# Hybrid streaming encoder step: the norm weight by one transfer into all partitions, first weight casts on other engines, late probabilities scaled on VectorE

## The chip, the cores and the metric

The kernel runs on one core of one Trainium2 chip. The metric is the device time of one launch in microseconds (us), the median of several runs; lower is better. TensorE multiplies matrices, VectorE (DVE in the profile) and ScalarE (ACT) work elementwise and read the accumulators in PSUM, GpSimd (POOL) works elementwise on SBUF, and SyncE (SP) issues nearly all transfers.

## The reference

One inference step of one layer over 2048 new frames of a prompt and 64 frames of a running stream, width 1024, all in float32:

```python
xn = rms_norm(x, ln_g)                       # ln_g: one weight per column, 1024 of them
aq, ak, av, ag, hq, hf, hi, hg = split(xn @ w_in)      # w_in 1024 x 4096, eight parts of 512 columns
# group A: 8 heads of 64, each chunk of 64 frames sees 576 keys, with a bias by distance
o_a = softmax(aq @ ak.T / 8 + bias) @ av * silu(ag)
# group B: 4 heads of 128, gated linear recurrence; lb comes from lb_gamma by a softmax
f = lb + (1 - lb) * sigmoid(hf)
S_t = diag(f_t) S_(t-1) + (1 - f_t) i_t^T ;  o_t = S_t^T silu(hq_t)
o_b = rms_norm(o, norm_g) * silu(hg)
y = rms_norm(x + concat(o_a, o_b) @ w_out, ln_f_g)
```

## The kernel before

**Stages.** The 2112 rows are worked in four superblocks (`SUPER`) of 512, 576, 512 and 512 rows. For each, the rows are normed and transposed (`x_tile`, `x_split`), 32 jobs project them onto 128 columns of `w_in` each (`project`, job lists `JOBS`), and for each group of heads attention (`attention`, `softmax_rows`, `attend`) and the recurrence (`recurrence`, `rec_block`) run between the projections. The output projection (`out_step`) multiplies by seven combinations of the quarters of `w_out`; it starts while the last superblock's attention still runs.

**Precision.** Each float32 product is made of three faster ones: a value is cast to a high half and the rest is its low half. So `x_split` casts the transposed rows to `xh` on ScalarE and subtracts to get `xl` on VectorE, and `w_split` casts a weight tile (128 x 1024) to its high half and subtracts its low half in four quarters on POOL. `project` then makes three passes of eight products: high weight with `xh`, high weight with `xl`, low weight with `xh`. Probabilities are treated alike: transposed on TensorE (`tr`), cast on ScalarE and subtracted on VectorE into `ph` (`split_p`), then multiplied with V (`pv`).

**Order.** Every piece is a generator ("thread"). A planner (`Plan`) runs them against an estimated clock: `yield "D", t` means go on when the estimated VectorE queue is near time t, `yield lambda: ...` means go on when a condition holds, and the set `have` carries marks that others wait for. What comes out is one fixed order of instructions for each engine; on the chip each engine runs its own in that order and waits at semaphores. A piece that is written later in the plan therefore stands later in its engine's queue, and a changed estimate can change the order of everything after it.

**The start.** `program()` issues the first transfers on SyncE: x tile 0, the norm weight `ln_in_g` as one row of 4 KB into partition 0 of `g_in` (the rest of `g_in` was filled with zeros by VectorE), x tile 1, weight 0, and so on. TensorE runs idle products with the identity (`spinning`, output `g`). When the row is there, two products of 512 columns with a matrix of ones spread it over all partitions into two PSUM banks, `s` and `pv` (each is two instructions in the trace); VectorE scales the first x tiles by row factor and by these banks (`scalar_tensor_tensor`, 512 columns at a time), and after the four tiles ScalarE copies the banks into `g_in` for the later superblocks. Each tile's row factor is a square with a row sum, a logarithm and an exponential on ScalarE. The first weight is cast by POOL, the next three by VectorE. The first two projections (`hq`, `hf` of head 0) run in halves of 256 rows.

**The forget bounds.** `forget_bounds` works out `lb` and `oml` in seven tiny instructions on VectorE and one exponential on ScalarE. The mark "bounds" is set after the first three of them, and `ev_f`, which evacuates the forget gate's accumulator `hf` (a first exponential on ScalarE frees it), waits for that mark.

**Late probabilities.** `softmax_exp` takes the exponential with its row sum on ScalarE, inverts the sum on VectorE, and scales the row by it on VectorE, as a `tensor_scalar`. After the mark "parts" (set by `out_rows_g` once the last superblock's recurrence is done, from where the output projection has its first weights) the scaling is done on ScalarE. That is the case for the last eight of them, 640 columns each.

Of the kernel before, what the change touches and what calls it, by code (L numbers as in the profile page):

```python
# [17 lines left out]
P = 128  # L18
# [354 lines left out]
def hymba_step(  # L373
# [110 lines left out]
    def forget_bounds():  # L484

        yield lambda: x_laid(0, 0, 1)
        yield "D", 0.0
        lmx = T(cst, [P, NHB], F32, "lmx")
        le = T(cst, [P, 2, NHB], F32, "le")
        dve.tensor_tensor(lmx, lbg[:, 0], lbg[:, 1], ALU.max)  # L490
        for i in range(2):
            dve.tensor_sub(le[:, i], lbg[:, i], lmx)
        t = C.dve()
        have.add("bounds")
        yield "A", t
        act.activation(le, le, AF.Exp)
        yield "D", C.act()
        dve.tensor_add(lmx, le[:, 0], le[:, 1])
        dve.reciprocal(lmx, lmx)
        dve.tensor_mul(lb, le[:, 0], lmx)  # L500
        dve.tensor_scalar(oml, lb, -1.0, 1.0, ALU.mult, ALU.add)
        sp.dma_start(g_norm, hg_norm_g)


# [36 lines left out]


    x_there = {}
    x_left = {(-1, 0): True, (-1, 1): True}

    def x_tile(sb, half, c, here=None, gain=None):
# [12 lines left out]
        ss = T(wk, [P, 1], F32, "ss", bufs=4)  # L559
        yield "A", t  # L560
        yield from tk["ck"].get()
        junk = T(wk, [P, D], mybir.dt.bfloat16, "ck", bufs=1)
        act.activation(junk[:rows], xn[:rows], AF.Square, accum_out=ss[:rows])
        tk["ck"].put()
        r = rstd_of(ss, rows, D)
        t = C.act()
        if (sb, c) == (0, P):
            have.add("factors")
        if not sb:
            yield lambda: "gain" in have and (not half or x_laid(0, 0, 1))  # L570
        yield "D", t
        t = []
        for k0 in (0, 4) if gain else (0,):
            cs = slice(k0 * P, k0 * P + (512 if gain else D))
            g = gain[k0 // 4] if gain else g_in[:rows]
            dve.scalar_tensor_tensor(xn[:rows, cs], xn[:rows, cs], r[:rows], g, ALU.mult, ALU.mult)
            t.append(C.dve())
        yield lambda: x_left.get((sb - 1, half), False)
        ends = []
        for k0 in (0, 4):  # L580
            yield t[min(k0 // 4, len(t) - 1)]
            tags = ("g", "tr") if sb else ("acc", "tr", "g", "pv")
# [12 lines left out]
        if (sb, half, c) == (0, 0, P):  # L595
            have.add("rows")
# [57 lines left out]

    def w_split(j, nt, raw, t, tok):
        yield "P", t
        yield lambda: j == 0 or j - 1 in w_at
        if j in (1, 2):
            yield lambda: x_laid(0, j - 1, 1) and "bounds" in have
        yield from tk["w"].get()  # L660
        w = w_pair()
        if j == 0:
            pool.tensor_copy(w[:, 0], raw)
            t = C.pool(700, t)
        else:
            dve.tensor_copy(w[:, 0], raw)
            t = C.dve(540, t)
        th = t
        yield "P", t
        for k in range(0, KT, 2):  # L670
            pool.tensor_sub(w[:, 1, k : k + 2], raw[:, k : k + 2], f32(w[:, 0, k : k + 2]))
            t = C.pool(320, t)
            if k == 0:
                w_at[j] = [w, th, []]
            w_at[j][2].append(t)
            if k < KT - 2:
                yield "P", t - 100.0
# [363 lines left out]
    def softmax_exp(s, nm, nk, out, t):  # L1041
        sm = T(wk, [P, 1], F32, "sm", bufs=4)
        act.activation(s[:, :nk], s[:, :nk], AF.Exp, bias=nm[:, 0:1], scale=-1.0, accum_out=sm)
        t = C.act(nk + 300, t)
        yield "D", t
        dve.reciprocal(sm, sm)
        t = C.dve()
        if "parts" in have:
            yield "A", t
            act.activation(s[:, :nk], s[:, :nk], AF.Copy, scale=sm)  # L1050
            t = C.act()
        else:
            dve.tensor_scalar(s[:, :nk], s[:, :nk], sm, None, ALU.mult)
            t = C.dve()
        out.append((s, t))

    def vcols(v, t, h, rows):
# [269 lines left out]
    def head_jobs(sb, h):  # L1327
# [18 lines left out]

        def ev_f(acc, off, bn, t):
            c = slice(off, off + bn)
            yield lambda: "bounds" in have and front()
            yield from tk["sig"].get()  # L1350
            yield "A", t
            f = T(wk, [P, 512], F32, "sig", bufs=2)
            act.activation(f[:, :bn], acc, AF.Exp, scale=-1.0)
            tk["acc"].put(1, C.act())
            act.activation(f[:, :bn], f[:, :bn], AF.Ln, bias=one_t)
            act.activation(f[:, :bn], f[:, :bn], AF.Exp, scale=-1.0)
            t = C.act(3.4 * bn, t)
# [12 lines left out]
            r.t = max(r.t, t)  # L1370
# [662 lines left out]
    def program():  # L2033


        dve.memset(g_in, 0.0)
        constants()
        kroom = f32(T(pa, [P, 2, WIN + NMAX], F32R, "kd")).rearrange("p a c -> p (a c)")
        vroom = f32(T(pa, [P, 9, 4, 64], F32R, "v")).rearrange("p t s d -> p (t s d)")
# [6 lines left out]
        landed = {}  # L2046
        for what, i in (("x", 0), ("g", 0), ("x", 1), ("w", 0), ("x", 2), ("w", 1), ("x", 3), ("b", 0), ("w", 2),
                        ("w", 3)):
            if what == "g":
                sp.dma_start(g_in[0:1], ln_in_g.rearrange("(o d) -> o d", o=1))  # L2050
            elif what == "b":
                sp.dma_start(lbg, lb_gamma)
            elif what == "x":
# [4 lines left out]
        for i in range(4):  # L2058
            raws[i] = (wr0[i], landed["w", i], "raw" if i < 2 else None)
        spin = psum("g")  # L2060
        gps = [s_ps()[:, 0], psum("pv")]
        tk["g"].take()
        tk["s_ps"].take()
        tk["pv"].take()
        C.now = 600.0
        C.free["P"] = 4000.0

        def first_x():
            for c in range(4):
                C.spawn(x_tile(0, c // 2, c * P, (xr0[c], landed["x", c]), gps), 0)  # L2070
            yield lambda: x_laid(0, 1, 1)
            tk["xn"].put(3, C.now)
            yield "A", C.now
            for a, tag in enumerate(("s_ps", "pv")):
                act.copy(g_in[:, a * 512 : a * 512 + 512], gps[a])
                tk[tag].put(1, C.act())
            for a in (f32(ql[64:128, 0]), f32(ql[0:64, 1]), asb[1]):
                yield "P", 0.0
                pool.memset(a, 0.0)
                C.pool(300)  # L2080
            yield lambda: 3 in w_at
            tk["kv"].put()
# [5 lines left out]
        C.spawn(first_x(), 0)  # L2088
        C.spawn(forget_bounds(), 1)
        C.spawn(weights(), 2)  # L2090
        for _ in range(7):
            spinning()
            yield None

        for a in range(2):
            pe.matmul(gps[a], f32(ones), g_in[:, a * 512 : a * 512 + 512], start=True, stop=True)
            yield None
        have.add("gain")
        while "rows" not in have:
            spinning()  # L2100
            yield None
# [190 lines left out]
```

## Time and profile before

| | us |
|---|---|
| median of 3 runs (lowest to highest) | 1266.81 (1264.8 to 1267.21) |
| the profiled execution | 1267.05 |
| its span, first to last instruction | 1265.3 |
| TensorE busy | 1245.4 |
| VectorE, ScalarE, POOL busy | 891.5, 707.4, 375.2 |

A line of the profile names engine, operation, output <- inputs, shape and count, then time; in a timeline the first number is the start, the second how long the merged instructions ran, and the bracket is the engine's idle time before them and what ended it. A row of waits has the sum, the count and the longest. A row by windows has, for each stretch, the busy us of TensorE, of its weight loads, of VectorE, ScalarE and POOL with instruction counts, then the granted clock, the share of the DMA engines and GB/s. All helpers record one line of the code (L266), so names of tiles tell operations apart.

### The profile page before, as it was taken

What the parts mean: (1) busy time and instruction counts of PE and PEld (TensorE: products, weight loads), DVE (VectorE), ACT (ScalarE), POOL (GpSimd) and SP (SyncE); (2) the same over time, 40 slices, a digit from 0 to 9 for tenths busy, and PEclk for the clock granted to TensorE, in tenths of its full rate; (3) what the DMA queues carried; (4) which work ended last, traced back from release to release, by engine and by line L of the source; (5) the groups of instructions that cost most, each with busy time, mean ns of one, the idle gap of its engine ahead of it and who ended that gap; (6) DMA issues with size and microseconds to landing.
All of it is one profiled execution on the core that took longest, in us unless ns stands there. A gap on an engine that the chain in (4) does not pass through costs nothing. (4 is left out here: it accounts for less than half of the span.)

```text
span 1265.3 us, 22177 instructions
## 1 busy us (share of the span) xinstructions
PE 1245.4 (98%) x8120; PEld 1084.0 (86%) x8120; DVE 891.5 (70%) x1854; ACT 707.4 (56%) x1548; POOL 375.2 (30%) x687
## 2 busy tenths in 40 slices
PE   8999999999999999999999999999999999999997
PEld 7788887899999999998888888998888888788786
DVE  6786869766857668687584748784848574578886
ACT  5363546665645557575565656763636454753443
POOL 6766665111110110101634635110101104451110
PEclk9999999999999999999999999999999999999999
DMA  7877777655353464545879597646363657886331
GB/s 258 318 271 248 262 274 279 219 180 199 128 191 127 166 214 157 190 153 193 277 244 313 210 352 257 235 147 234 127 229 117 228 187 272 317 282 207 125 133 67
DMA packets 94830, 271.72 MB, mean 215 GB/s; under 512 B 10305, under 2 KB 43073, under 8 KB 77058
## 3 DMA queue, kind: packets, MB, share of 16 engines
q1 hardware_dynamic: 94722, 270.31, 60.7%
q8 instruction: 64, 1.05, 0.3%
q14 instruction: 44, 0.36, 0.1%
HBM read 186.66 MB, written 83.62 MB: 214 GB/s over the span
## 5 line engine op out<-in xcount | busy, mean ns | idle before, releaser
L266 PE MATMUL acc<-xh,w 128*128 128x512 f32 (+2 forms) x2720 | 567.4, 347 | 1.0 <-ACT sig L266 0.8
L266 PEld LDWEIGHTS acc<-xh,w 128*128 128x128 f32 x2720 | 436.1, 189 | 52.2 <-issue 1.9
L266 PE MATMUL acc<-xl,w 128*128 128x512 f32 (+2 forms) x1360 | 298.0, 348 | 0.0
L266 PEld LDWEIGHTS acc<-xl,w 128*128 128x128 f32 x1360 | 219.6, 189 | 24.8 <-issue 0.5
L266 POOL TENSOR_TENSOR mixa<-mixa,sga 128x256 f32<-128x256 f32 (+1 forms) x36 | 30.2, 840 | 352.1 <-DVE mixa L266 279.9
L266 DVE CUSTOM_DVE_ANT_0 pr<-s,bias 128x640 f32<-128x640 f32 (+5 forms) x144 | 100.7, 703 | 35.3 <-PE s L266 34.8
L266 ACT ACTIVATE pr<-pr,nm 128x640 f32<-128x640 f32 (+4 forms) x132 | 100.8, 763 | 38.2 <-DVE nm L266 37.2
L266 ACT CAST ph<-tr 128x512 fp32r<-128x512 f32 (+3 forms) x176 | 88.1, 508 | 60.1 <-PE tr L266 29.0
L266 POOL TENSOR_TENSOR w<-wraw,w 128x256 fp32r<-128x256 f32 x120 | 105.4, 907 | 48.4 <-DVE w L266 32.7
L266 DVE TENSOR_TENSOR ph<-tr,ph 128x512 fp32r<-128x512 f32 (+3 forms) x176 | 100.9, 589 | 9.4 <-ACT ph L266 8.2
L266 PE MATMUL pv<-ph,v 128*128 128x256 f32 (+2 forms) x344 | 97.5, 373 | 3.1 <-DVE ph L266 2.4
L266 PE MATMUL tr<-ident,pr 128*128 128x128 f32 x580 | 90.8, 273 | 1.8 <-DVE sig L266 0.7
L266 PEld LDWEIGHTS tr<-ident,pr 128*128 128x128 f32 x580 | 70.3, 140 | 16.0 <-issue 3.8
L266 ACT ACTIVATE sig<-acc 128x256 f32<-128x256 f32 (+2 forms) x86 | 42.8, 498 | 72.9 <-PE acc L266 72.6
L266 DVE TENSOR_SCALAR pr<-pr,sm 128x640 f32<-128x640 f32 (+3 forms) x124 | 68.6, 553 | 4.4
L266 DVE TENSOR_TENSOR mixa<-mixa,pv 64x256 f32<-64x256 f32 (+1 forms) x144 | 56.8, 394 | 20.8 <-ACT mixa L266 16.7
L266 ACT COPY vT<-acc 128x512 f32<-128x512 f32 (+2 forms) x64 | 31.2, 488 | 66.6 <-PE acc L266 66.5
L266 PEld LDWEIGHTS pv<-ph,v 128*128 128x128 f32 (+1 forms) x344 | 57.3, 189 | 10.9 <-issue 2.0
L266 ACT ACTIVATE sig<-sig 128x512 f32<-128x512 f32 (+2 forms) x109 | 57.3, 527 | 10.0 <-DVE gk L266 7.3
L266 POOL TENSOR_TENSOR k<-ob 128x512 f32<-128x512 f32 (+2 forms) x20 | 17.8, 891 | 145.4 <-ACT ob L266 145.4
L266 PE MATMUL s<-kd,q 128*128 128x320 f32 (+3 forms) x232 | 56.9, 315 | 0.1
L266 POOL TENSOR_TENSOR xn<-wraw,xn 128x256 fp32r<-128x256 f32 x48 | 37.8, 803 | 61.9 <-ACT xn L266 61.8
(315 smaller groups left out, 2100.7 us busy)
## 6 DMA issues: line engine op xcount, KB each, us to landing
w<-wd SPq DMA_DIRECT2D x96, 1024.0 KB, 5.0
wd<-w SPq DMA_DIRECT2D x32, 1024.0 KB, 7.3
wraw<-in_w_in_dram SPq DMA_DIRECT2D x30, 512.0 KB, 5.4
wod<-xn SPq DMA_DIRECT2D x28, 512.0 KB, 4.2
xn<-in_x_prompt_dram SPq DMA_DIRECT2D x23, 512.0 KB, 5.5
bias<-biasd SPq DMA_DIRECT2D x12, 640.0 KB, 7.1
carry<-kd SPq DMA_DIRECT2D x12, 512.0 KB, 7.9
carry<-v SPq DMA_DIRECT2D x12, 512.0 KB, 5.3
```

Of the source, the lines that this page charges most:

```text
L266: r = f(*args, **kw)
```

## The change

Three things, in one change:

1. The norm weight is read by one transfer with a source step of zero into all 128 partitions of `g_in` (512 KB written), after x tile 1 instead of before it. The zero fill, the four products, the two PSUM banks held for them and the two copies into `g_in` go. The first four tiles are scaled from `g_in` in SBUF, still in two halves.
2. The first weight's cast goes from POOL to VectorE, after the scaling of the second x tile (mark "scaled"). The third and fourth weights' casts go from VectorE to ScalarE. The evacuation of the forget gate waits, in the plan, for a new mark "lb", set when `lb` and `oml` are written.
3. After "parts", the scaling of probabilities is a VectorE `tensor_tensor` with the inverse sum spread along the row by a step of zero, in place of ScalarE's copy with a scale.

```diff
         dve.tensor_scalar(oml, lb, -1.0, 1.0, ALU.mult, ALU.add)
+        have.add("lb")
...
-            yield lambda: "gain" in have and (not half or x_laid(0, 0, 1))
+            yield lambda: not half or x_laid(0, 0, 1)
+            t = max(t, landed["g", 0])
         yield "D", t
         t = []
-        for k0 in (0, 4) if gain else (0,):
-            cs = slice(k0 * P, k0 * P + (512 if gain else D))
-            g = gain[k0 // 4] if gain else g_in[:rows]
-            dve.scalar_tensor_tensor(xn[:rows, cs], xn[:rows, cs], r[:rows], g, ALU.mult, ALU.mult)
+        for k0 in (0,) if sb else (0, 4):
+            cs = slice(k0 * P, k0 * P + (D if sb else 512))
+            dve.scalar_tensor_tensor(xn[:rows, cs], xn[:rows, cs], r[:rows], g_in[:rows, cs], ALU.mult, ALU.mult)
             t.append(C.dve())
+        if (sb, c) == (0, P):
+            have.add("scaled")
...
-        yield lambda: j == 0 or j - 1 in w_at
+        yield lambda: j - 1 in w_at if j else "scaled" in have
         if j in (1, 2):
             yield lambda: x_laid(0, j - 1, 1) and "bounds" in have
         yield from tk["w"].get()
         w = w_pair()
-        if j == 0:
-            pool.tensor_copy(w[:, 0], raw)
-            t = C.pool(700, t)
+        if j in (2, 3):
+            yield "A", t
+            act.copy(w[:, 0], raw)
+            t = C.act()
         else:
             dve.tensor_copy(w[:, 0], raw)
-            t = C.dve(540, t)
+            t = C.dve()
...
         if "parts" in have:
-            yield "A", t
-            act.activation(s[:, :nk], s[:, :nk], AF.Copy, scale=sm)
-            t = C.act()
+            dve.tensor_tensor(s[:, :nk], s[:, :nk], sm.to_broadcast([P, nk]), ALU.mult)
         else:
             dve.tensor_scalar(s[:, :nk], s[:, :nk], sm, None, ALU.mult)
-            t = C.dve()
+        t = C.dve()
...
-            yield lambda: "bounds" in have and front()
+            yield lambda: "lb" in have and front()
...
-        dve.memset(g_in, 0.0)
...
-        for what, i in (("x", 0), ("g", 0), ("x", 1), ("w", 0), ("x", 2), ("w", 1), ("x", 3), ("b", 0), ("w", 2),
+        for what, i in (("x", 0), ("x", 1), ("g", 0), ("w", 0), ("x", 2), ("w", 1), ("x", 3), ("b", 0), ("w", 2),
                         ("w", 3)):
             if what == "g":
-                sp.dma_start(g_in[0:1], ln_in_g.rearrange("(o d) -> o d", o=1))
+                sp.dma_start(g_in, ln_in_g.rearrange("(o d) -> o d", o=1).broadcast_to([P, D]))
...
-        gps = [s_ps()[:, 0], psum("pv")]
-        tk["s_ps"].take()
-        tk["pv"].take()
...
-            yield "A", C.now
-            for a, tag in enumerate(("s_ps", "pv")):
-                act.copy(g_in[:, a * 512 : a * 512 + 512], gps[a])
-                tk[tag].put(1, C.act())
...
-        for _ in range(7):
-            spinning()
-            yield None
-
-        for a in range(2):
-            pe.matmul(gps[a], f32(ones), g_in[:, a * 512 : a * 512 + 512], start=True, stop=True)
-            yield None
-        have.add("gain")
         while "rows" not in have:
             spinning()
             yield None
```

More of the change, by code (lines that the diff above doesn't have):

```diff
@@ L543, in hymba_step, with x_tile @@
     x_there = {}
+    landed = {}
     x_left = {(-1, 0): True, (-1, 1): True}
-    def x_tile(sb, half, c, here=None, gain=None):
+    def x_tile(sb, half, c, here=None):
         off, bn = SUPER[sb][3][half]
@@ L2045, in program @@
                 tk[tag].take()
-        landed = {}
-        for what, i in (("x", 0), ("g", 0), ("x", 1), ("w", 0), ("x", 2), ("w", 1), ("x", 3), ("b", 0), ("w", 2),
+        for what, i in (("x", 0), ("x", 1), ("g", 0), ("w", 0), ("x", 2), ("w", 1), ("x", 3), ("b", 0), ("w", 2),
                         ("w", 3)):
             if what == "g":
-                sp.dma_start(g_in[0:1], ln_in_g.rearrange("(o d) -> o d", o=1))
+                sp.dma_start(g_in, ln_in_g.rearrange("(o d) -> o d", o=1).broadcast_to([P, D]))
             elif what == "b":
@@ L2069, in first_x @@
             for c in range(4):
-                C.spawn(x_tile(0, c // 2, c * P, (xr0[c], landed["x", c]), gps), 0)
+                C.spawn(x_tile(0, c // 2, c * P, (xr0[c], landed["x", c])), 0)
             yield lambda: x_laid(0, 1, 1)
             tk["xn"].put(3, C.now)
-            yield "A", C.now
-            for a, tag in enumerate(("s_ps", "pv")):
-                act.copy(g_in[:, a * 512 : a * 512 + 512], gps[a])
-                tk[tag].put(1, C.act())
             for a in (f32(ql[64:128, 0]), f32(ql[0:64, 1]), asb[1]):
```

## The prediction

> **What bounds the kernel now.** I read the shares of busy time first, then the waits of TensorE, then the two places where the change works: the first 25 us and the stretch from 1075 to 1108 us. The page gives the shares:
>
> ```profile
> PE 1245.4 (98%) x8120; PEld 1084.0 (86%) x8120; DVE 891.5 (70%) x1854; ACT 707.4 (56%) x1548; POOL 375.2 (30%) x687
> ```
>
> TensorE is busy 98% of the span. The change takes away no product of the reference, so it can only gain where TensorE waits, or where what it does is filler. The waits of TensorE over the whole run begin like this (sum in us, times, longest):
>
> ```profile
> PE pv L266 <- DVE ph L266: 2.4, 2, 1.4
> PE g L266 <- POOL one L266: 1.4, 1, 1.4
> PE g L266 <- DVE xl L266: 1.2, 5, 0.4
> PE s L266 <- DMA gin<-in_ln_in_g_dram: 1.2, 1, 1.2
> PE g L266 <- DVE asb L266: 1.0, 1, 1.0
> PE acc L266 <- ACT sig L266: 0.8, 1, 0.8
> ```
>
> Two of these rows lie under the change: the gain's transfer (1.2) and the late products of the probabilities with V, which wait for VectorE's low halves `ph` (2.4 in two waits). At the start more is lost than waits show, because the idle products with the identity ("g") count as busy. The timeline of TensorE shows when real work begins:
>
> ```profile
> 5.97 2.05 PE L266 MATMUL s<-gin,ones 128*128 128x512 f32 x2 [1.18 <-DMA gin<-in_ln_in_g_dram]
> 7.80 1.92 PE L266 MATMUL pv<-gin,ones 128*128 128x512 f32 x2
> ...
> 13.40 1.19 PE L266 MATMUL acc<-xh,w 128*128 128x256 f32 x8 [0.28 <-issue]
> 14.43 1.12 PE L266 MATMUL acc<-xl,w 128*128 128x256 f32 x8
> ```
>
> The first projection starts at 13.40. What leads to it is VectorE's chain:
>
> ```profile
> 1.09 0.91 DVE L266 MEMSET gin<- 128x1024 f32 x1 [1.09 <-PEq L2279]
> ...
> 8.13 0.75 DVE L266 SCALAR_TENSOR_TENSOR xn<-xn,rstd,s 128x512 f32<-128x512 f32 x1 [5.11 <-PE s L266]
> 9.76 0.75 DVE L266 SCALAR_TENSOR_TENSOR xn<-xn,rstd,pv 128x512 f32<-128x512 f32 x1 [0.88 <-PE pv L266]
> 10.42 0.74 DVE L266 SCALAR_TENSOR_TENSOR xn<-xn,rstd,s 128x512 f32<-128x512 f32 x1
> 11.08 0.74 DVE L266 SCALAR_TENSOR_TENSOR xn<-xn,rstd,pv 128x512 f32<-128x512 f32 x1
> 12.02 1.29 DVE L266 TENSOR_TENSOR xl<-acc,xh 128x512 fp32r<-128x512 f32 x2 [0.19 <-ACT xh L266]
> 13.34 1.29 DVE L266 TENSOR_TENSOR xl<-tr,xh 128x512 fp32r<-128x512 f32 x2
> ...
> 14.88 0.69 DVE L266 CAST w<-wraw 128x1024 fp32r<-128x1024 f32 x1
> ```
>
> Four scalings, one every 0.66 us when nothing stops them, the last ending at 11.82; then four subtractions of low halves, one every 0.65 us, the last ending at 14.63. Between the first two scalings VectorE waits 0.88 us for the second half of the spread gain. So the start is set by when the gain stands in all partitions, and after that by VectorE.
>
> **Part 1, the gain.** Four products and a zero fill go; the gain now comes as 512 KB. SyncE's queue and ScalarE show the transfers before:
>
> ```profile
> 0.81 0.39 SPq L266 DMA_DIRECT2D xn<-in_x_prompt_dram  x1
> 2.03 0.31 SPq L266 DMA_DIRECT2D gin<-in_ln_in_g_dram  x1
> 2.39 0.35 SPq L266 DMA_DIRECT2D xn<-in_x_prompt_dram  x1
> ```
>
> ```profile
> 7.09 1.06 ACT L266 ACTIVATE ck<-xn 128x1024 bf16<-128x1024 f32 x1 [1.25 <-DMA xn<-in_x_prompt_dram]
> ...
> 20.45 0.59 ACT L266 COPY gin<-s 128x512 f32<-128x512 f32 x1
> 20.93 0.60 ACT L266 COPY gin<-pv 128x512 f32<-128x512 f32 x1
> 21.41 0.41 ACT L266 ACTIVATE sig<-acc 128x256 f32<-128x256 f32 x1
> ```
>
> ```profile
> 8.35 1.04 POOL L266 CAST w<-wraw 128x1024 fp32r<-128x1024 f32 x1 [4.75 <-DMA wraw<-in_w_in_dram]
> ```
>
> The gain's issue at 2.03 stood behind the zero fill (1.09 + 0.91 = 2.00), and the second tile of x and everything else on SyncE stood behind it. Without the fill the second x tile goes out where the first's issue ends, 0.81 + 0.39 = 1.2, or a little after: 1.1 us sooner. It landed at 7.09, so now at about 6.0, or nearer 5.3 if its bytes follow the first tile's without a pause. The first weight tile landed at 8.35, 1.26 after it: that is one 512 KB transfer at the rate of the row 7.00 to 8.50 below (columns at the right: clock, DMA share, GB/s). For a row of DRAM read into all partitions the trace has one case, the final gain:
>
> ```profile
> gin<-in_ln_f_g_dram SPq DMA_DIRECT2D x1, 512.0 KB
> ```
>
> ```profile
> 7.00:8.50 1.50, 1.50 (x3) 0.63 (x2) 0.37 (x1) 1.37 (x3) 0.15 (x1) 1.00 1.01 410
> 1075.50:1076.50 1.00, 1.00 (x6) 0.82 (x5) 0.75 (x2) 0.21 (x1) 0.00 (x0) 1.00 0.90 249
> 1076.50:1078.75 2.25, 2.25 (x14) 1.95 (x13) 0.98 (x3) 1.98 (x4) 0.00 (x0) 1.00 0.95 230
> ```
>
> It was issued behind a 256 KB store. The first stretch moves 0.25 MB, that store; the second moves 2.25 x 230 = 0.52 MB, the gain, with all engines of the DMA busy at little more than half the rate. I read the boundary from bytes and queue order, since no instruction marks it. So the gain takes 1.28 us at best and 2.25 us by its own kind. It lands between 5.3 + 1.28 = 6.6 and 6.0 + 2.25 = 8.2; I take 5.3 + 2.25 = 7.6, the rate of its own kind behind an x tile that no longer waits. The last of four scalings then ends at 7.6 + 3 x 0.66 + 0.75 = 10.3, 1.5 us earlier than 11.82. At 8.2 it is 0.9, at 6.6 it would be 2.5.
>
> **Part 2, the casts.** The first weight's high half leaves POOL (1.04) and goes to VectorE (0.69), behind the four scalings. Its transfer lands behind 512 KB more: between 8.35 - 1.1 + 1.28 = 8.5 and 8.35 + 2.25 = 10.6, about when VectorE gets there (10.3) or sooner. The cast ends at about 11.0, and POOL's four low quarters start after it and not at 9.4; they are wanted only in the third pass of the projection, two passes of about 1.0 us after the start, each by its own quarter, so I cost that at nothing. If POOL's train were late there, it would cost up to 0.7, one quarter. Since the cast stands ahead of the four subtractions, these end at 11.0 + 4 x 0.65 = 13.6 against 14.63: only 1.0 us earlier, while the first projection can start at 11.1, 2.3 earlier than 13.40, and then waits for the low halves. I take 1.4 us for TensorE from both, near VectorE's end, because after this VectorE has hardly a pause until 24 us. With the bounds of the landing: 0.4 to 2.2.
>
> The casts of the third and fourth weights move from VectorE to ScalarE. There is no such instruction in the trace; the nearest is the 1024-wide square at 7.09, 1.06 us, so about 2.1 us for both. The two copies of the gain (20.45 and 20.93, 0.48 apart) go. At 21.41 ScalarE reads the accumulator for which TensorE waits 0.8 us. One cast ahead of it stands for the two copies, no change; both ahead cost 1.1; none gives 0.2, what is left being the end of the product itself and the exponential. I take 0. The evacuation now also waits in the order until the forget bounds' last step is written; those are four tiny instructions on VectorE, so it costs nothing unless the order of the queue turns, which the 1.1 covers.
>
> **Part 3, the late probabilities.** Eight scalings by the inverse sum move from ScalarE to VectorE:
>
> ```profile
> L266 ACT ACTIVATE pr<-pr,sm x8: 814/830/832, 1077.4 to 1106.8; 128x640 f32<-128x640 f32 x8
> L266 DVE TENSOR_TENSOR pr<-pr,acc x7: 673/681/689, 1139.4 to 1258.7; 128x512 f32<-128x512 f32 x7
> ```
>
> ```profile
> 1093.21 1.55 ACT L266 ACTIVATE pr<-pr,sm 128x640 f32<-128x640 f32 x2
> ```
>
> ```profile
> 1092.00:1108.00 16.00, 14.57 (x77) 12.04 (x76) 8.61 (x22) 12.68 (x26) 12.55 (x21) 1.00 0.84 335
> ```
>
> ScalarE loses 8 x 0.83 = 6.6 us. VectorE gains 8 times a two-input instruction of 640 columns; the 512-column row is 0.681, so 0.681 x 640/512 = 0.85, together 6.8 us. In the windowed row (busy us of TensorE, its weight loads, VectorE, ScalarE, POOL) ScalarE works 12.68 of 16 and VectorE 8.61: the load goes from the fuller to the emptier queue. Both waits for `ph` (2.4 us together) stand behind ScalarE: VectorE subtracts what ScalarE has cast, and ahead of that an addition needs a bank that ScalarE copies. At the second wait two scalings, 1.55 us, stood in ScalarE's queue ahead of those casts. I expect half of the 2.4 to go, 1.2 us: the bank cannot be copied before its product has ended, so not all of it goes unless the order changes too. Bounds: 2.4 gained; below nothing, 1.5 lost, if a scaling (0.85) stands ahead of the subtraction in both places and costs most of its length.
>
> A rule that speaks against this part stands behind a row. The same VectorE operation of two inputs in SBUF takes two times:
>
> ```profile
> L266 DVE TENSOR_TENSOR q<-q,gq x3: 673/674/1229, 35.0 to 150.0; 128x512 f32<-128x512 f32 x3
> ```
>
> The Trainium skill, "SBUF — State Buffer", section "SBUF: two separate sides", says that VectorE with two SBUF inputs and GpSimd reading SBUF exclude each other for a whole instruction; the 1229 beside 673 agrees, and by it this part would lose instead of gain.
>
> **The sum.** The profiled execution took 1267.05 us, its span being 1265.3. Start 1.4, casts two and three 0, late part 1.2: 2.6 us less, 1264.45. The median of the runs shown is 1266.81, 0.24 below the profiled one, so 1264.2. The order of every queue is worked out by the kernel's own planner from estimated times, so all of it may shift a little; the smaller waits in the rows above show what one change of order is worth, 0.2 to 1.2 us, either way. I put 1.2 us either way on the sum for that.
>
> **The rivals.**
>
> *Hidden (no measurable change).* The start's gain is taken back. TensorE waits for the recurrence (DVE asb, 1.0); if that chain doesn't come sooner, TensorE only reaches it sooner and waits longer. For it: VectorE, not the gain, feeds the first projections. Against: the recurrence's own inputs come from the same shifted products. Then 0.4 of the 1.4 is left, and with 0.5 of the late 1.2: 1267.05 - 0.24 - 0.9 = 1265.9.
>
> *Slower: VectorE and POOL shut each other out late.* From 1092 to 1108 POOL works 12.55 of 16 us; before 1088 it is nearly idle, so this touches the last four of the eight scalings. By the row 673/674/1229 an instruction of that kind grows by up to 0.56, and POOL's subtraction behind it waits for 0.85. The place is the second wait for `ph`. Each of four scalings ahead of the subtraction then costs 0.85 + 0.56 = 1.4 on VectorE's chain. VectorE has 16 - 8.61 = 7.4 us free there and would use 5.6 of it, so it decides only if the scalings stand right before the subtractions for which TensorE waits. Then the 1.2 turns into 4 x 1.4 = 5.6 less the free time in front of two of them (2 x 0.9) = 3.8 lost; with the start's 1.4: 1266.8 + 2.4 = 1269.2. It decides once two of the four stand so.
>
> *The broadcast doesn't pay.* The transfer could be worse than its late sister, behind three others at once. Landing at 9.5 would put the last scaling at 12.2, later than 11.82. Start then -0.4 and, with the cast ahead of the subtractions, up to 1.0 lost; with late 1.2 gained: 1266.6.
>
> **How the numbers follow.** What measurements of this kernel can tell from no change is about 0.2%, 2.5 us. Both parts pay, as in the sum: 0.52, and that is faster by just over 0.2%, with more room below than above, since the landing's better bound (2.2) and both waits for `ph` (2.4) are worth 0.8 + 1.2 more. Hidden: 0.24, and the broadcast that doesn't pay: 0.08, both within. The lock, or an order that turns against the kernel by as much: 0.16, slower. The range: 0.8 + 1.2 + 1.2 below 1264.2 is 1261.0, taken as 1261.2; above it reaches to the lock's 1269.2, taken as 1269.0.
>
> **What would show it.** In the changed profile: the first scaling on VectorE at 7.6 (6.6 to 8.2), four of them without the 0.88 pause; the first projection at 11.1 to 11.9 and its low pass at 13.0 to 13.6; the cast of `w` on VectorE behind the scalings; 1024-wide casts of about 1.06 on ScalarE near 20; the wait of TensorE for `sig` still 0.7 to 0.9. Late: eight VectorE instructions of about 0.85, those after 1092 up to 1.4, and the waits for `ph` at 1.2 in sum. Wrong would be: a first scaling later than 9, a wait for `sig` of 1.5 or more, waits for `ph` above 2.4, or new waits between 25 and 1070 us that outweigh all of this.

## The result and the profile after

| | before | after |
|---|---|---|
| median of 22 runs each, same chip (us) | 1265.11 | 1267.74 |
| lowest to highest | 1263.73 to 1268.32 | 1266.33 to 1270.08 |
| the profiled execution, its span | 1267.05, 1265.3 | 1269.08, 1267.4 |

After to before: 1.0019, interval 1.0012 to 1.0026. The change is slower by 0.19%, some 2.4 us; the forecast was 2.6 us faster. The time lies in the stated range (1261.2 to 1269.0), the sign is the other one.

The page of after, shares of busy time (ScalarE has less, VectorE more, TensorE the same):

```profile
PE 1246.1 (98%) x8130; PEld 1085.9 (86%) x8130; DVE 903.7 (71%) x1862; ACT 703.2 (55%) x1540; POOL 375.9 (30%) x681
```

Waits of TensorE in after, whole run, the head of the list (sum, times, longest):

```profile
PE acc L266 <- DVE xn L266: 2.3, 2, 2.0
PE pv L266 <- ACT pr L266: 2.2, 1, 2.2
PE g L266 <- POOL one L266: 1.4, 1, 1.4
PE g L266 <- DVE xl L266: 1.2, 5, 0.4
PE g L266 <- DVE k L266: 1.2, 1, 1.2
```

Two rows are new. The gain's row and the `ph` row of before are gone; in their places stand a wait for the scaled x tile (2.0 at the start) and one of `pv` (2.2 near the end). Timelines of after, first VectorE and POOL, then TensorE, then SyncE's queue and ScalarE:

```profile
8.90 2.74 DVE L266 SCALAR_TENSOR_TENSOR xn<-xn,rstd,gin 128x512 f32<-128x512 f32 x4 [6.01 <-DMA gin<-in_ln_in_g_dram]
...
16.38 1.89 DVE L266 SCALAR_TENSOR_TENSOR xn<-xn,rstd,gin 128x512 f32<-128x512 f32 x2
18.20 2.37 DVE L266 SCALAR_TENSOR_TENSOR kd<-kd,rstd,gin 128x512 f32<-128x512 f32 x2
16.54 4.62 POOL L266 TENSOR_TENSOR w<-wraw,w 128x256 fp32r<-128x256 f32 x4 [0.77 <-DVE w L266]
```

```profile
9.71 0.66 PE L266 MATMUL acc<-ident,xn 128*128 128x128 f32 x4 [2.00 <-DVE xn L266]
...
12.99 1.19 PE L266 MATMUL acc<-xh,w 128*128 128x256 f32 x8 [0.64 <-ACT xh L266]
14.10 1.34 PE L266 MATMUL acc<-xl,w 128*128 128x256 f32 x8
```

```profile
0.81 0.86 SPq L266 DMA_DIRECT2D xn<-in_x_prompt_dram  x2
1.71 0.43 SPq L266 DMA_DIRECT2D gin<-in_ln_in_g_dram  x1
...
21.86 1.05 ACT L266 CAST w<-kd 128x1024 fp32r<-128x1024 f32 x1
22.82 1.04 ACT L266 CAST w<-v 128x1024 fp32r<-128x1024 f32 x1
23.77 0.38 ACT L266 ACTIVATE sig<-acc 128x256 f32<-128x256 f32 x1
```

The gain is issued 0.3 us earlier than its 4 KB row was, but VectorE, idle for 6.01 us, can use it only from 8.90; the forecast was 7.6 (6.6 to 8.2). The four scalings then run without a pause, and the first projection starts at 12.99. The windows show the transfer:

```profile
3.00:4.00 1.00, 1.00 (x7) 1.00 (x6) 0.00 (x0) 0.00 (x0) 0.47 (x1) 1.00 0.98 377
4.00:5.00 1.00, 1.00 (x6) 1.00 (x6) 0.00 (x0) 0.94 (x1) 0.00 (x0) 1.00 0.95 270
5.00:6.00 1.00, 1.00 (x6) 1.00 (x6) 0.00 (x0) 0.87 (x5) 0.00 (x0) 1.00 0.80 164
6.00:7.00 1.00, 1.00 (x11) 1.00 (x10) 0.00 (x0) 0.97 (x3) 0.00 (x0) 1.00 0.93 238
7.00:8.00 1.00, 0.72 (x7) 0.53 (x5) 0.00 (x0) 0.41 (x2) 0.00 (x0) 1.00 0.99 344
```

From 4 to 7 us the rate falls (270, 164 and 238 GB/s against 377 before it), as it did for the final gain (230). Between 5 and 7 only 0.40 MB move, and weight 0, issued 0.5 us behind the gain, shares what follows.

### The profile page after: what moved, and what is told of

It is laid out like the page before. It is cut to its first block, busy times and chain, and to the rows that moved or that the text cites. A ratio compares the mean times of both kernels' runs of the same rounds, so it can differ in the third digit from the quotient of the medians.

```text
span 1267.4 us, 22191 instructions
## 1 busy us (share of the span) xinstructions
PE 1246.1 (98%) x8130; PEld 1085.9 (86%) x8130; DVE 903.7 (71%) x1862; ACT 703.2 (55%) x1540; POOL 375.9 (30%) x681
## 3 DMA queue, kind: packets, MB, share of 16 engines
q8 instruction: 64, 1.05, 0.3%
## 4 chain that ended last, share of the span: by engine, by line
PE 84%; DVE 5%; POOL 3%; DMA 3%; ACT 2%; issue 2%; SPq 0%; DVEq 0%; POOLq 0%; ACTq 0%
PE acc L266 61%; PE g L266 7%; PE tr L266 6%; PE s L266 5%; PE pv L266 5%; POOL w L266 2%; DVE xn L266 1%; DMA xn<-in_x_prompt_dram 1%; DMA ck<-in_cache_attn_k_dram 1%; DVE pr L266 1%; DMA gin<-in_ln_in_g_dram 1%; ACT sig L266 0%; DMA wraw<-in_w_in_dram 0%; DVE xl L266 0%; DMA wd<-w 0%
```

## The experiments

All ratios are to before, with a 95% interval, runs of before on the same chip. "Start" means the first projection's first product.

**The parts by themselves.** `e1_late_only` is before with the late scaling on VectorE (its edit is shown), `e2_start_only` is after with the late scaling back on ScalarE:

```diff
-            yield "A", t
-            act.activation(s[:, :nk], s[:, :nk], AF.Copy, scale=sm)
+            dve.tensor_tensor(s[:, :nk], s[:, :nk], sm.to_broadcast([P, nk]), ALU.mult)
```

> The kernel before with the late part alone (eight probabilities scaled on VectorE), nothing changed at the start. Theory A (the late part loses): VectorE's two-input scalings grow to 1.0 to 1.4 us beside POOL, stand ahead of the additions that free the PSUM bank of the products with V, TensorE waits about 2 us once and its clock drops for one stretch of 3.4 us: 1 us slower than before, between 0.3 and 2.0. Theory B (the late part pays, the start loses everything): the two waits for the low halves go, 1 us faster than before.

> The changed kernel with the late part undone (scaled on ScalarE as before). Theory A: only the start's loss is left, 0.7 us slower than before (0.3 to 1.2). Theory B: 2.5 us slower than before, as the whole change or worse.

`e3_gain_only` is before with the transfer into all partitions (casts as before), `e4_casts_only` before with the casts moved. Both keep the new mark "lb". Of each edit the main lines:

```diff
-                sp.dma_start(g_in[0:1], ln_in_g.rearrange("(o d) -> o d", o=1))
+                sp.dma_start(g_in, ln_in_g.rearrange("(o d) -> o d", o=1).broadcast_to([P, D]))
```

```diff
-        if j == 0:
-            pool.tensor_copy(w[:, 0], raw)
-            t = C.pool(700, t)
+        if j in (2, 3):
+            yield "A", t
+            act.copy(w[:, 0], raw)
...
```

> The kernel before with the norm weight's transfer into all partitions, the casts of the first weights where they were (the mark for the forget bounds is kept, since the plan is not valid without it). Theory A (the transfer and the scalings from SBUF lose): first scaling at 8.9, the scalings of the third and fourth tile at 0.9 to 1.2 us each beside POOL, 0.7 us slower than before. Rival (the casts lose): 0.3 us faster to equal.

> The kernel before with the casts moved alone (first weight on VectorE behind the scalings, third and fourth on ScalarE), the norm weight still spread by products. Theory A (the transfer loses, not the casts): within 0.3 us of before. Rival (the casts lose): 0.7 us slower or more, by low halves of x that stand behind the cast and by two casts ahead of the forget gate's exponential.

| kernel | ratio | start in its profile |
|---|---|---|
| late part alone | 0.9997 (0.9987 to 1.0008) | 10.53 |
| start alone | 1.0019 (1.0010 to 1.0027) | 12.40 |
| gain alone | 1.0025 (1.0011 to 1.0039) | 13.31 |
| casts alone | 1.0003 (0.9994 to 1.0011) | 11.27 |

The loss goes with the gain's transfer; the casts and the late part are neutral within their intervals. The third column holds a surprise: the late part alone has the start of before, instruction for instruction, and starts at 10.53, where the profile of before says 13.40.

**The kernel before once more, and without its idle products.** `e12_before_again` is before unchanged. `e8_no_spin` takes out the seven idle products ahead of the spreading ones:

```diff
-        for _ in range(7):
+        for _ in range(0):
             spinning()
```

> The kernel before, unchanged, for a second profile. Theory A (the profile from which the prediction was made had its two spreading products at half clock by chance of the clock gate's windows): with full clock the products take 0.59 to 0.70 each and the first projection starts at 10.4 to 11.0. Rival B (before always starts late, and the earlier starts of the other kernels come from their edits): products of 1.06 again and the first projection at 13.4.

> The kernel before without the seven idle products ahead of the two that spread the norm weight. Theory A (the products were slow in the profile shown because TensorE's clock had not risen): they take 1.06 us each again, the first projection starts at about 13.4, and it is 2 to 2.5 us slower than before. Rival (the clock at the start does not matter, x tile 2 sets the start): within 0.5 us of before.

The spreading products and the start, by the timelines of the second profile of before and of the late part alone:

```profile
5.21 1.71 PE L266 MATMUL s<-gin,ones 128*128 128x512 f32 x2 [0.42 <-DMA gin<-in_ln_in_g_dram]
6.75 1.02 PE L266 MATMUL pv<-gin,ones 128*128 128x512 f32 x2
...
10.92 1.19 PE L266 MATMUL acc<-xh,w 128*128 128x256 f32 x8 [0.28 <-ACT xh L266]
```

```profile
5.15 1.24 PE L266 MATMUL s<-gin,ones 128*128 128x512 f32 x2 [0.37 <-DMA gin<-in_ln_in_g_dram]
6.23 1.02 PE L266 MATMUL pv<-gin,ones 128*128 128x512 f32 x2
```

A pair takes 1.02 at its usual length, and took 2.05 and 1.92 in the profile that the prediction read (1061 to 1193 ns each). In the second profile they became fast inside the first pair (grouped by form: 727 and 1190 ns, then 592 each). That the slow ones ran at half clock is read from their length alone: the granted clock of the windows is 1.00 in both profiles there. Where it is 0.50, from 10 to 13 us of `e14_gain_other_plan` below, four transposes take 1.06, which take 0.60 at 1.00; 1061 to 592 is nearly the same ratio. The Trainium skill, "TensorE: Matmul & The Clock Gate", section "What's actually happening", says that TensorE starts at half clock, that it is raised after a busy window of about 3.4 us, and that these windows run free, so the moment differs from run to run; that the three profiles became fast at different moments agrees.

Of four profiles with this same start (before, second before, late part alone, and `e10_late_ts` below) two had the slow products: 13.40, 10.92, 10.53, 12.64, mean 11.87. Theory A holds for the start, though not for all of the gap: of the 2.5 us between the two profiles of before, 0.8 is the 4 KB row, which TensorE waited for until 5.97 in one and 5.21 in the other. Nor does the whole gap reach the end: those two executions took 1267.05 and 1266.22. Without the idle products the pairs took 2.05 and 1.91 but began at 4.27, the start was 12.01, and the ratio 1.0010 (1.0000 to 1.0020): the direction was as expected, the size half of it.

**The gain's landing.** `e5_no_gain` replaces the transfer by a fill of ones on VectorE: the norm weight is left out of the first norm. `e7_gain_first` issues the transfer ahead of the x tiles, `e11_gain_halves` makes two transfers of 512 columns of it.

```diff
-                sp.dma_start(g_in, ln_in_g.rearrange("(o d) -> o d", o=1).broadcast_to([P, D]))
+                dve.memset(g_in, 1.0)
+                landed[what, i] = C.dve()
+                continue
```

```diff
-        for what, i in (("x", 0), ("x", 1), ("g", 0), ("w", 0), ...
+        for what, i in (("g", 0), ("x", 0), ("x", 1), ("w", 0), ...
```

```diff
-                sp.dma_start(g_in, ln_in_g.rearrange("(o d) -> o d", o=1).broadcast_to([P, D]))
+                for k0 in (0, 512):
+                    sp.dma_start(g_in[:, k0 : k0 + 512], ln_in_g[k0 : k0 + 512].rearrange("(o d) -> o d", o=1).broadcast_to([P, 512]))
```

> The changed kernel without the norm weight's transfer: its tile is filled with ones by VectorE, so the weight is left out of the first norm. Theory A (the landing of the 512 KB sets the start): the first scaling comes with the first tile's row factor at 5.9 us instead of 8.9, the second tile's at about 7.4, the first projection at 10 to 10.5 instead of 13.0; 2 to 2.5 us faster than the changed kernel, so equal to before or up to 0.5 us faster. Rival (what loses is VectorE's order and the SBUF scalings beside POOL): the first scaling comes sooner but the first projection's low pass is less than 1 us sooner; 1.5 us slower than before or more.

> The changed kernel with the norm weight's transfer issued first, ahead of both x tiles. Theory A (place in the queue decides when it lands): it lands near 5 us, the first x tile near 6, the second near 7.3; first scaling at about 7.7, the second tile's at 9.2, the first projection at about 12; 0.7 us faster than the changed kernel. Rival (a source step of zero is slow wherever it stands and holds up what is behind it): x tiles land 2 us later than that, and it is as slow as the changed kernel or slower.

> The change as it is, but the gain's transfer issued as two of 512 columns each (256 KB each), one behind the other. Theory A (the bytes of the spread transfer set the start: 512 KB at some 230 GB/s behind two x tiles): the first scaling at 7.0 to 7.6 and the second at 8.7 to 9.2, the last of four ending at 10.5 to 11.0 against 11.6 in the change; time 0.5 to 1 us below the change, still 1 to 2 us above before, ratio 1.0008 to 1.0015. Rival B (it is the time from issue to landing that is long, whatever the bytes): first scaling at 8.5 or later, time as the change, 1.002.

Without the transfer the start is 10.23 and the ratio 0.9994 (0.9985 to 1.0003): the loss is gone, and even a gain that costs nothing makes the kernel no faster than before by a measurable amount. With the gain first, x tile 0 pays (ScalarE's timeline, then VectorE's):

```profile
6.64 1.06 ACT L266 ACTIVATE ck<-xn 128x1024 bf16<-128x1024 f32 x1 [4.56 <-DMA xn<-in_x_prompt_dram]
...
8.45 1.41 DVE L266 SCALAR_TENSOR_TENSOR xn<-xn,rstd,gin 128x512 f32<-128x512 f32 x2 [5.57 <-ACT rstd L266]
```

The start is at 12.82, hardly better than after's 12.99, yet the ratio is 1.0000 (0.9990 to 1.0009). Two halves bring the first scaling no sooner (8.64, start 13.39), yet 1.0001 (0.9992 to 1.0009). So the start alone does not say what the run takes. Each of these kernels also has another order of instructions, since the planner counts the transfer differently: with the gain first and with two halves in all queues, without the transfer in VectorE's and TensorE's alone.

**Landing and order crossed.** `e13_no_gain_same_plan` fills the gain with ones as above (the norm weight is left out again) but lets the planner count the transfer, so that all queues keep after's order. `e14_gain_other_plan` makes the transfer but lets the planner count the fill, which gives the order of the kernel without the gain. `e15_after_again` is after. By the traces the two orders differ in little: after's has the first weight's cast between the first two low halves on VectorE, the other has it ahead of both, and a dozen of TensorE's products before 24 us stand elsewhere; apart from fills and idle products, all else on VectorE, ScalarE, POOL and TensorE is in the same order.

```diff
-                sp.dma_start(g_in, ln_in_g.rearrange("(o d) -> o d", o=1).broadcast_to([P, D]))
+                row = ln_in_g.rearrange("(o d) -> o d", o=1).broadcast_to([P, D])
...
+                dve.eng.memset(g_in, 1.0)
+                C.charge("S", sp.cost("dma_start", [there, row], {}), [there], [row])
```

```diff
-                sp.dma_start(g_in, ln_in_g.rearrange("(o d) -> o d", o=1).broadcast_to([P, D]))
...
+                sp.eng.dma_start(g_in, ln_in_g.rearrange("(o d) -> o d", o=1).broadcast_to([P, D]))
+                C.charge("D", dve.cost("memset", [there], {}), [there], [])
+                landed[what, i] = C.dve()
...
```

> The change with the gain filled with ones by VectorE instead of read (the norm weight is left out of the first norm), but with the planner told that the transfer is made: every queue keeps the change's order, apart from the one fill and the one transfer. Theory A (the loss is the late landing of the gain itself): the first scaling near 5.9 and the first projection at 10.2 to 10.6, 2.4 to 2.8 before the change; the time falls by 1.5 to 2.8 us, ratio to before 0.9995 to 1.0007. Rival B (the loss is in the order that the planner makes when it counts the transfer, in waits later on): the start comes sooner but the time stays near the change, ratio 1.0012 to 1.0022.

> The change with the real transfer of the gain, but with the planner told that VectorE fills it: the order of every queue is that of the kernel without the gain (which took 0.9994 of before). Theory A (the late landing is the loss): first scaling at 8.3 to 8.9 and the time 1.5 to 2.8 us above the kernel without the gain, ratio to before 1.0008 to 1.0018. Rival B (the order is the loss): the start is late but the time stays at 0.999 to 1.0003 of before, since that order takes the delay up in later waits.

> The changed kernel, unchanged, on the same chip as the two other kernels of this batch and for a second profile. Theory A and rival B both: ratio to before 1.0012 to 1.0026, first scaling at 8.3 to 8.9, the wait of pv for the late scaling of pr near 2.2. If that wait is followed by a stretch at half clock of some 3.4 us again, the profile shows it near 1105; without it the time should be near 1266.8 and not 1267.7.

| | gain by transfer | gain at once |
|---|---|---|
| after's order | 1.0019 (1.0008 to 1.0030) | 1.0000 (0.9989 to 1.0010) |
| the other order | 1.0005 (0.9995 to 1.0016) | 0.9994 (0.9985 to 1.0003), in another batch |

First scalings and starts of the three, by their timelines (the transfer in after's order, none in that order, the transfer in the other):

```profile
8.35 2.74 DVE L266 SCALAR_TENSOR_TENSOR xn<-xn,rstd,gin 128x512 f32<-128x512 f32 x4 [5.46 <-DMA gin<-in_ln_in_g_dram]
...
12.44 1.19 PE L266 MATMUL acc<-xh,w 128*128 128x256 f32 x8 [0.64 <-ACT xh L266]
```

```profile
6.02 1.42 DVE L266 SCALAR_TENSOR_TENSOR xn<-xn,rstd,gin 128x512 f32<-128x512 f32 x2 [2.35 <-ACT rstd L266]
...
10.38 1.18 PE L266 MATMUL acc<-xh,w 128*128 128x256 f32 x8 [0.64 <-ACT xh L266]
```

```profile
8.42 2.74 DVE L266 SCALAR_TENSOR_TENSOR xn<-xn,rstd,gin 128x512 f32<-128x512 f32 x4 [5.53 <-DMA gin<-in_ln_in_g_dram]
...
13.23 1.50 PE L266 MATMUL acc<-xh,w 128*128 128x256 f32 x8
```

The third start is late for one more reason: in that profile the granted clock was 0.50 from 10 to 13 us, after TensorE had waited 1.91 for the scaled tile. With after's order held, the landing moves the start by 2.06 (12.44 to 10.38) and the median by 2.27 (1268.53 to 1266.26): what is lost at the start is lost at the end. By the table the landing costs 0.19% and 0.11% in the two orders, on average 0.15% +- 0.10, 1.9 us; after's order costs 0.14% and 0.06%, on average 0.10% +- 0.10, 1.3 us. So theory A has the larger share; the share of the order is not clear of zero. One wait of TensorE between 13 and 80 us, for `k` of the recurrence's first block, is a candidate for where an order would lose it:

```profile
PE g L266 <- DVE k L266: 1.7, 1, 1.7
```

```profile
PE g L266 <- DVE k L266: 0.7, 1, 0.7
```

This wait is 1.2 and 0.8 in the two profiles of after, 1.7 (first fence) in after's order with the gain at once, 0.7 (second) in the other order with the transfer, 0.8 in that order with the gain at once, and 0.5 in the second profile of before. Two profiles of one kernel differ by 0.4 here, so where the order loses, if it does, stays open.

**The scalings of tiles 3 and 4.** In after they take 1.89 and 2.37 per two, beside a POOL that takes 4.62 for four quarters. `e6_gain_psum` copies the gain into the two PSUM banks on ScalarE and scales these tiles from there:

```diff
-            dve.scalar_tensor_tensor(xn[:rows, cs], xn[:rows, cs], r[:rows], g_in[:rows, cs], ALU.mult, ALU.mult)
+            dve.scalar_tensor_tensor(xn[:rows, cs], xn[:rows, cs], r[:rows], gps[k0 // 4] if gps else g_in[:rows, cs], ALU.mult, ALU.mult)
...
+                act.copy(gps[a], g_in[:, a * 512 : a * 512 + 512])
```

> The changed kernel, with the norm weight copied by ScalarE from SBUF into two PSUM banks once it has landed, and the third and fourth x tile scaled from there. Theory A (scalings with both tensors in SBUF and POOL's subtractions shut each other out): these four scalings take 0.74 each in place of 1.9 and 2.4 us for pairs, POOL's four quarters of the second weight 2.8 in place of 4.6; 1.0 us (0.3 to 1.5) faster than the changed kernel. Rival (TensorE is not held by them): the same instructions shrink and the time stays within 0.3 us of the changed kernel, 2.4 us slower than before.

```profile
16.32 0.73 DVE L266 SCALAR_TENSOR_TENSOR xn<-xn,rstd,s 128x512 f32<-128x512 f32 x1
...
16.48 2.81 POOL L266 TENSOR_TENSOR w<-wraw,w 128x256 fp32r<-128x256 f32 x4 [0.78 <-DVE w L266]
```

The scalings are back at 0.73 each and POOL's quarters at 2.81, so the two engines did hold each other up. The ratio is 1.0027 (1.0017 to 1.0037): no better. That TensorE did not wait for these instructions is likely but not shown alone, since the two copies on ScalarE and the banks held for them also change the order of every queue.

**The late part.** `e10_late_ts` is before with the late scaling on VectorE as a `tensor_scalar`, which has one tensor input:

```diff
-        if "parts" in have:
-            yield "A", t
-            act.activation(s[:, :nk], s[:, :nk], AF.Copy, scale=sm)
...
+        dve.tensor_scalar(s[:, :nk], s[:, :nk], sm, None, ALU.mult)
```

> Before with the late scaling of probabilities on VectorE as a tensor_scalar (one tensor input and a factor per row) and not as a tensor_tensor with a spread factor; start as before. Theory A (the late part is neutral because the longer VectorE instructions beside POOL, 1.0 to 1.4 us, only move a wait from ph to the pv bank): instructions of 0.45 to 0.6 us that do not grow beside POOL, no new wait of TensorE for the exponentials' scaling above 1 us between 1100 and 1108, no stretch at half clock after it, time 1 to 3 us below before, ratio 0.998 to 0.999. Rival B (it is the place in VectorE's queue and not the length that makes the wait): the wait of pv for pr stays at 1.5 us or more and the time stays within 0.1% of before.

First the late stretch of after, the eight scalings grouped by form, then VectorE's timeline and TensorE's:

```profile
L266 DVE TENSOR_TENSOR pr<-pr,sm x8: 824/918/1382, 1078.1 to 1105.4; 128x640 f32<-128x640 f32 x8
```

```profile
1100.98 1.38 DVE L266 TENSOR_TENSOR pr<-pr,sm 128x640 f32<-128x640 f32 x1
1102.28 0.81 DVE L266 CUSTOM_DVE_ANT_0 pr<-s,bias 128x640 f32<-128x640 f32 x1
...
1103.03 0.68 DVE L266 TENSOR_TENSOR xn<-xn,acc 128x512 f32<-128x512 f32 x1
1103.73 0.88 DVE L266 TENSOR_TENSOR mixa<-mixa,pv 64x256 f32<-64x256 f32 x2
```

```profile
1104.76 0.81 PE L266 MATMUL pv<-ph,v 128*128 128x512 f32 x2 [2.17 <-ACT pr L266]
1105.37 1.06 PE L266 MATMUL acc<-xh,slot 128*128 128x512 f32 x2
1106.22 1.06 PE L266 MATMUL pv<-ph,v 128*128 128x512 f32 x2
```

The `pv` bank has one buffer, and it comes free only with the two `mixa` instructions, which now stand behind a scaling of 1.38, a score reduction and an addition. The row names ScalarE's `pr`; in the late part alone the same wait (2.20) is put down to `DVE mixa`. And after the wait two matmuls take 1.06 where two take 0.62 in the second run of the changed kernel, after a wait just as long (2.18):

```profile
1105.47 0.70 PE L266 MATMUL pv<-ph,v 128*128 128x512 f32 x2 [2.18 <-ACT pr L266]
1106.01 0.62 PE L266 MATMUL acc<-xh,slot 128*128 128x512 f32 x2
1106.47 0.63 PE L266 MATMUL pv<-ph,v 128*128 128x512 f32 x2
```

The windows behind that wait, after first, then its second profile (the granted clock is the third number from the right):

```profile
1105.00:1108.50 3.50, 3.50 (x10) 2.70 (x10) 1.82 (x5) 0.63 (x3) 3.50 (x8) 0.53 0.94 352
1105.50:1109.00 3.50, 3.50 (x21) 3.02 (x22) 2.04 (x5) 1.32 (x4) 3.50 (x7) 1.00 0.98 368
```

3.5 us at about half clock are some 1.7 us lost. Nine profiles have this wait of 2.2: five show such a stretch within 2 us of it (after, `e6`, `e11`, `e13`, `e14`), four do not (second after, `e1`, `e5`, `e7`), and none of the eight profiles without the wait shows one there. The runs' mean clocks fit in part: the changed kernel's second batch took 1267.4 at 0.999 (4 runs), 1268.6 at 0.998 (3) and 1269.9 at 0.997 (5); the late part alone 1265.3 at 0.999 (5), 1265.1 at 0.998 (4) and 1268.1 at 0.997 (3). But a mean does not say where in the run the clock was low: in the profile of the late part alone (0.998) the one low stretch lies behind TensorE's last product, where it costs nothing.

In `e10_late_ts` one input was no cure:

```profile
L266 DVE TENSOR_SCALAR pr<-pr,sm x8: 553/554/1633, 1077.4 to 1104.4; 128x640 f32<-128x640 f32 x8
```

0.55 while POOL is idle, but 1.63 and 1.01 beside it. Theory A fails in its instructions. The times split: five runs from 1263.2 to 1265.6 at a clock of 0.998 or 0.999, seven from 1270.8 to 1275.8 at 0.994 to 0.996; together 1.0025 (1.0001 to 1.0049). The profiled execution is of the first kind and shows no half-clock stretch late (its longest late wait is 1.05). What the other kind loses, some 10 us, no profile here shows.

**Before with the two x tiles first.** `e9_swap` issues x tile 1 ahead of the 4 KB row, all else as before:

```diff
-        for what, i in (("x", 0), ("g", 0), ("x", 1), ("w", 0), ...
+        for what, i in (("x", 0), ("x", 1), ("g", 0), ("w", 0), ...
```

> Before with only the order of the first transfers changed: x tile 0, x tile 1, the 4 KB row of the gain, weight 0. The gain stays a 4 KB row, spread by the four products. Theory A (the start is set by when the gain stands in all partitions; in the executions whose spreading products run at full clock it already starts near 10.5, and the second x tile's factor, whose square stands at 6.6 in the late-part-only kernel, is what comes last there): the second square comes 0.8 earlier, at 5.8, the first projection between 9.7 and 10.5, and the time is 0.3 to 0.9 below before, ratio 0.9993 to 0.9998, too little to be told from none. Rival B (the swap of the transfers is what makes the change slow, by pushing the gain behind 512 KB): the gain's row lands about 1 us later, the first projection 1 us later, time 0.5 to 1 above before.

The start came at 10.29, the second square at 6.24 (5.8 expected), and the ratio is 0.9995 (0.9986 to 1.0004). That is the earliest start with the real gain, and no difference in time that these runs can tell. No kernel here is measurably faster than before.

## Why the prediction was wrong, point by point

**The base of the sum.** The first projection "at 13.40" was one draw. Four profiles of that start average 11.87, so some 1.5 us of the gap that the change was to close were not there in the mean of these profiles. The row that showed it was quoted: the two spreading pairs of 2.05 and 1.92, each followed by VectorE, were taken as their price. This step failed first.

**Part 1, the landing.** 7.6 was forecast; six profiles with the whole transfer (after twice, start alone, gain alone, PSUM, other order) show the first scaling at 8.90, 8.35, 8.31, 8.57, 8.85 and 8.42, all above the stated 8.2. The rate was about right (164 to 246 GB/s between 5 and 7 us in these profiles, 230 forecast): by the windows the bytes of both x tiles and of the gain could have moved by 6.9 to 7.3, if weight 0 had moved none. The 1.4 to 1.6 us from there to the scaling, in which weight 0 shares the engines and the last bytes become a release, had no term; the traces do not part the two. The second x tile was no later than 5.74, where its square follows the first without a wait. Mean 8.57, 1.0 late. The start in the two profiles of after is 12.7 on average, 0.85 later than 11.87, where the sum had 1.4 to gain. The bounds put on that term, 0.4 to 2.2, were also not those of the landing: 0.6 later or 1.0 sooner than 7.6 makes it 0.8 to 2.4. "Broadcast doesn't pay" had the mechanism, but against the wrong base: it needed a landing at 9.5, and 8.6 was enough.

**Part 2, the casts.** Zero was forecast for them, 1.0003 measured. Both late casts (1.05 and 1.04, 1.06 forecast) do stand ahead of the exponential at 23.77, the 1.1 bound's case, but TensorE has no wait of 0.8 for `sig` any more. The later start is not the reason: the wait is gone too in the kernel without the transfer, whose start is at 10.23, and with the casts alone, at 11.27. What took it away is not shown.

**The scalings from SBUF** were priced at 0.66 for all tiles. That held for the first two (0.66 apart, POOL idle), not for the others (1.89 and 2.37 per two, first start to last end). The quoted rule on SBUF was applied to the late part only. What it cost the run was not enough to show: with the copy into PSUM the ratio was no better.

**Part 3, the late part.** Both `ph` waits (2.4) went, more than the 1.2 forecast, and the instructions are as priced (0.82, up to 1.38; 0.85 and 1.4 forecast). What failed is that nothing was put down for what is late next: a wait of 2.2 for the `pv` bank, and behind it in five profiles of nine a half-clock stretch worth some 1.7. By the ratio of 0.9997 some 0.4 us were gained, against 1.2 forecast. The lock rival described this place, but its price of 3.8 was too high: it counted four scalings of 1.4 ahead of the subtraction, and in the trace one of 1.38 stands ahead of the two `mixa` instructions.

**Order.** 1.2 either way was put on it. The crossed runs give 1.3, with an interval that reaches down to zero; they compare two orders of the changed kernel, not after's with before's.

Together, as an estimate from these numbers: 1.4 forecast at the start and 0.85 lost, 2.3; the late part, 0.8; the order, about 1.3, if it stands for before's order too: 4.4 of the 5.0 us between -2.6 and +2.4. That is within what the intervals allow.

## What to carry to other kernels

Before an early gap is taken as a price, look whether the instructions in it run at their usual length: a matmul of 1061 ns that takes 592 in another profile of the same kernel belongs to that execution, and one profile of before is then no base. A transfer of one row into all partitions replaces a few products only if it lands before the products would have ended, and its landing must include what shares the engines with it. Where a wait is taken away, follow the one-buffer bank behind it: an instruction that grows ahead of the one that frees the bank gives the wait back.

## What the runs showed of the hardware

A wait of 2.2 us was enough for the clock to fall: from 1105 the granted clock was 0.53 for some 3.4 us in one execution, and 1.00 after the same wait in another execution of the same program. It fell after that wait in five profiles of nine, and after the wait of 1.9 to 2.4 at the start in one of seven (`e14_gain_other_plan`). The Trainium skill, "TensorE: Matmul & The Clock Gate", section "Why this matters for your kernels", has gaps of over about 3 us lower it; here a shorter one did, in some executions.

A VectorE `tensor_scalar` with one tensor input in SBUF was not spared beside POOL either: 0.55 became 1.63.
